# Fused RMSNorm and SiLU on one core: loads and stores alternate between two DMA queues

## The chip, the cores and the metric

The kernel runs on one core of a Trainium2 chip. The metric is the device time of one execution in microseconds (us); less is better. Before the change three executions took 316.88, 316.94 and 317.01 us, a median of 316.94 us. A measurement of this kernel can tell a difference of about 0.2% (0.63 us) from no change.

## The reference

The input x has 8 x 1024 rows of 2048 float32 values, gamma has 2048 values and eps is one number:

```python
rms = np.sqrt(np.mean(x ** 2, axis=-1, keepdims=True) + eps)
out = gamma * x / rms
return (out * (1 / (1 + np.exp(-out)))).astype(np.float32)
```

So each row is scaled by the reciprocal of its root mean square and by gamma, and then goes through SiLU. Input and output are 64 MiB each, and each byte has to cross between the chip's memory and the core's SBUF once.

## The kernel before

**Tiles.** The 8192 rows are cut into 16 blocks of 512 rows. One block is one tile `xt` of 128 partitions x 8192 values (four rows of 2048 values in each partition, `J = 4`), 4 MiB, and the whole block is moved by one DMA in each direction. A partition's part is 32 KB. The pool has six tiles (`BUFS = 6`), so a block's tile can be loaded again only after the store of the block that held it has landed. All the work on a block is done in place in its tile.

**Work on a block.** `squares_scalar` (L65) squares and sums the first one or two rows of each partition on ScalarE (ACT); `squares_vector` (L73) does the others on VectorE (DVE). `share(b)` gives ACT one row in the even blocks 4 to 12 and two elsewhere. `root` (L82, ACT) takes the square root, `invert` (L87, DVE) the reciprocal, `multiply` (L92, DVE) four row products with the reciprocal and gamma, and `silu` (L98, ACT) two halves of SiLU, after which it calls `store`. The last block has its own ending: four products with gamma (L155, DVE), four SiLUs that apply the reciprocal (L157, ACT), and its store.

**Queues.** `load` (L54) issues on ACT's DMA queue, which the profile calls q10 and ACTq. `store` (L102) issues on SyncE's, called q1 and SPq. SyncE (SP) does nothing else but one load of gamma (L110). In each engine instructions run in the order written, and the order is written out by hand (`tc.manual_schedule()`): an instruction that waits holds up all that stand behind it on its engine.

**Order.** Loads 0 to 5 are issued at the start (0 and 1 at once, 2 to 5 after gamma has been spread over the partitions with the help of TensorE). The main loop runs over b = 0 to 14. For b from 3 to 13 an iteration is

```python
squares_scalar(b + 1, loads)   # loads = [b + 3]: issued after the first row's squares
squares_vector(b + 1)
root(b + 1)
multiply(b)
silu(b)                        # ends with store(b)
invert(b + 1)
```

For b < 3 and b = 14 `multiply(b)` comes first and `silu(b)` stands between the two kinds of squares. Load k is issued in iteration k - 3, on ACT, and waits there until the store of block k - 6 has landed.

Of the kernel before, what the change touches and what calls it, by code (L numbers as in the profile page):

```python
# [1 line left out]

# [4 lines left out]

ACT = mybir.ActivationFunctionType
ALU = mybir.AluOpType


@with_exitstack
def kernel(
    ctx: ExitStack,
    tc: tile.TileContext,
    x: bass.AP,
    gamma: bass.AP,
    eps: bass.AP,
    out: bass.AP,
):  # L20

    nc = tc.nc
    P = nc.NUM_PARTITIONS
    f32 = mybir.dt.float32
    x2 = x.flatten_outer_dims()
    o2 = out.flatten_outer_dims()  # L30
    n, d = x2.shape
    J = 4
    BUFS = 6
    nblk = n // (P * J)
    xb = x2.rearrange("(b p j) d -> b p (j d)", p=P, j=J)
    ob = o2.rearrange("(b p j) d -> b p (j d)", p=P, j=J)

    singles = ctx.enter_context(tc.tile_pool(name="singles", bufs=1))
    pool = ctx.enter_context(tc.tile_pool(name="pool", bufs=BUFS))
    small = ctx.enter_context(tc.tile_pool(name="small", bufs=2))  # L40
    psum = ctx.enter_context(tc.tile_pool(name="psum", bufs=1, space=bass.MemoryType.PSUM))

    Q = 4
    w = d // Q
    g = singles.tile([P, d], f32)
    eps_t = singles.tile([P, 1], f32)
    ones = singles.tile([P, P], f32)
    junk_a = psum.tile([P, d], f32, name="junk_a")
    junk_v = psum.tile([P, d], f32, name="junk_v")
    blocks, sss, rmss, rstds = {}, {}, {}, {}  # L50

    def load(b):
        xt = pool.tile([P, J * d], f32, name="xt")
        nc.scalar.dma_start(out=xt, in_=xb[b])  # L54
        blocks[b] = xt

    def row(b, j):
        return blocks[b][:, j * d:(j + 1) * d]

    def squares_scalar(b, loads=()):  # L60


        sss[b] = small.tile([P, J], f32, name="ss")
        for j in range(share(b)):
            nc.scalar.activation(out=junk_a, in_=row(b, j), func=ACT.Square,  # L65
                                 accum_out=sss[b][:, j:j + 1])
            if j == 0:
                for s in loads:
                    load(s)

    def squares_vector(b):
        for j in range(share(b), J):
            nc.vector.tensor_tensor_reduce(  # L73
                out=junk_v, in0=row(b, j), in1=row(b, j), scale=1.0, scalar=0.0,
                op0=ALU.mult, op1=ALU.add, accum_out=sss[b][:, j:j + 1])

    def share(b):
        return 1 if 4 <= b <= 12 and b % 2 == 0 else 2

    def root(b):  # L80
        rms = small.tile([P, J], f32, name="rms")
        nc.scalar.activation(out=rms, in_=sss.pop(b), func=ACT.Sqrt, scale=1.0 / d, bias=eps_t)  # L82
        rmss[b] = rms

    def invert(b):
        rstd = small.tile([P, J], f32, name="rstd")
        nc.vector.reciprocal(out=rstd, in_=rmss.pop(b))  # L87
        rstds[b] = rstd

    def multiply(b):  # L90
        for j in range(J):
            nc.vector.scalar_tensor_tensor(out=row(b, j), in0=row(b, j), scalar=rstds[b][:, j:j + 1],  # L92
                                           in1=g, op0=ALU.mult, op1=ALU.mult)

    def silu(b):
        for h in range(0, J, 2):
            cols = slice(h * d, (h + 2) * d)
            nc.scalar.activation(out=blocks[b][:, cols], in_=blocks[b][:, cols], func=ACT.Silu)  # L98
        store(b)

    def store(b):
        nc.sync.dma_start(out=ob[b], in_=blocks[b])  # L102

    with tc.manual_schedule():

        load(0)
        nc.vector.memset(ones, 1.0)  # L107
        nc.vector.memset(eps_t, float(eps))
        nc.scalar.activation(out=junk_a[:, 0:1], in_=ones[:, 0:1], func=ACT.Square)  # L109
        nc.sync.dma_start(out=g[0:1, :], in_=bass.AP(tensor=gamma.tensor, offset=gamma.offset, ap=[[d, 1], [1, d]]))  # L110
        for c in range(Q):
            cols = slice(c * w, (c + 1) * w)
            nc.tensor.matmul(junk_v[:, cols], ones[0:1, :], g[0:1, cols], start=True, stop=True)  # L113
        load(1)
        nc.vector.tensor_copy(out=g, in_=junk_v)  # L115
        nc.scalar.copy(out=junk_a[:, 0:1], in_=junk_v[:, d - 1:d])  # L116
        for b in range(2, BUFS):
            load(b)

        last = nblk - 1
        SOON = 3
        squares_scalar(0)
        squares_vector(0)
        root(0)
        invert(0)
        for b in range(last):
            loads = [b + 3] if BUFS <= b + 3 < nblk else []
            if b < SOON:  # L130
                multiply(b)
                squares_scalar(b + 1, loads)
                silu(b)
                squares_vector(b + 1)
                root(b + 1)
            elif b < last - 1:
                squares_scalar(b + 1, loads)
# [3 lines that stand above are left out]
                silu(b)  # L141
            else:
                multiply(b)
                squares_scalar(b + 1)
                silu(b)
                squares_vector(b + 1)
                root(b + 1)
            if b + 1 < last:
                invert(b + 1)


        for j in range(J):
            if j == J // 2:
                invert(last)
            nc.vector.tensor_mul(out=row(last, j), in0=row(last, j), in1=g)  # L155
        for j in range(J):
            nc.scalar.activation(out=row(last, j), in_=row(last, j), func=ACT.Silu,  # L157
                                 scale=rstds[last][:, j:j + 1])
        store(last)


# [1 line left out]
_INS = ['x', 'gamma', 'eps']  # L163
_OUTS = [((8, 1024, 2048), 'float32')]

_NUMBERS = {'eps': 9.999999747378752e-06}


# [26 lines left out]
```

## Time and profile before

| | us |
|---|---|
| median of three executions (316.88 to 317.01) | 316.94 |
| span of the profiled execution (its own time is not listed apart; the median is 1.8 longer than the span) | 315.1 |
| DVE busy (75%) | 235.3 |
| ACT busy (68%) | 213.9 |
| PE busy (2%) | 7.2 |
| median of a load from issue to landing, 16 of 4096 KB | 38.7 |
| median of a store from issue to landing, 16 of 4096 KB | 29.0 |
| load 14: issued, landed | 221.2, 259.9 |
| load 15: issued, landed | 240.6, 279.2 |
| store 13: issued, landed | 277.4, 294.9 |
| store 14: issued, landed | 290.3, 304.6 |
| store 15: issued, landed | 300.9, 314.3 |

Read it so: the span is that of one execution under the profiler, and all durations below are of that execution. "DMA share" is the mean busy share of the core's 16 DMA engines; in a short window it can pass 1, because a packet is counted whole in the window in which it starts. A "landing" is the moment at which the transfer's semaphore is complete.

### The profile page before, as it was taken

What the parts mean: (1) busy time and instruction counts of PE and PEld (TensorE: products, weight loads), DVE (VectorE), ACT (ScalarE), POOL (GpSimd) and SP (SyncE); (2) the same over time, 40 slices, a digit from 0 to 9 for tenths busy, and PEclk for the clock granted to TensorE, in tenths of its full rate; (3) what the DMA queues carried; (4) which work ended last, traced back from release to release, by engine and by line L of the source; (5) the groups of instructions that cost most, each with busy time, mean ns of one, the idle gap of its engine ahead of it and who ended that gap; (6) DMA issues with size and microseconds to landing.
All of it is one profiled execution on the core that took longest, in us unless ns stands there. A gap on an engine that the chain in (4) does not pass through costs nothing.

```text
span 315.1 us, 439 instructions
## 1 busy us (share of the span) xinstructions
PE 7.2 (2%) x8; PEld 2.5 (1%) x8; DVE 235.3 (75%) x157; ACT 213.9 (68%) x137; POOL 0.2 (0%) x4
## 2 busy tenths in 40 slices
PE   6200000000000000000000000000000000000000
PEld 2000000000000000000000000000000000000000
DVE  0679697979895695957969489593995939999600
ACT  1269998972799258682687827877278768779910
POOL 0000000000000000000000000000000000000000
DMA  8999999999999999999999999999999999999997
GB/s 334 412 453 416 383 458 408 462 403 462 403 459 408 454 412 458 408 462 403 462 403 462 408 458 408 458 408 458 416 449 416 449 416 449 428 437 428 437 428 308
DMA packets 4613, 134.24 MB, mean 426 GB/s; under 512 B 514, under 2 KB 514, under 8 KB 514
## 3 DMA queue, kind: packets, MB, share of 16 engines
q10 hardware_dynamic: 2304, 67.11, 49.8%
q1 hardware_dynamic: 2306, 67.12, 49.3%
q14 instruction: 3, 0.02, 0.0%
HBM read 67.12 MB, written 67.11 MB: 426 GB/s over the span
## 4 chain that ended last, share of the span: by engine, by line
DMA 68%; DVE 14%; ACT 11%; issue 1%; ACTq 1%; DVEq 0%
DMA xt<-in_x_dram 68%; DVE xt L92 9%; DVE junk_v L73 5%; ACT xt L98 4%; ACT junk_a L65 3%; ACT xt L157 2%; ACT L82 1%; ACTq L190 1%; ACT L157 0%; ACT L98 0%; ACT rms L82 0%; DVE ss L73 0%; ACTq L54 0%; DVE rstd L87 0%; ACT L109 0%
## 5 line engine op out<-in xcount | busy, mean ns | idle before, releaser
L92 DVE SCALAR_TENSOR_TENSOR xt<-xt,rstd,g 128x2048 f32<-128x2048 f32 x60 | 137.0, 2346 | 0.1
L98 ACT ACTIVATE xt<-xt 128x4096 f32<-128x4096 f32 x30 | 108.3, 3615 | 27.4 <-DVE xt L92 27.4
L73 DVE CUSTOM_DVE_ANT_0 junk_v<-xt 128x2048 f32<-128x2048 f32 x37 | 85.1, 2299 | 42.9 <-DMA xt<-in_x_dram 42.2
L65 ACT ACTIVATE junk_a<-xt 128x2048 f32<-128x2048 f32 x27 | 50.7, 1876 | 16.1 <-DMA xt<-in_x_dram 14.0
L82 ACT ACT_TABLE_LOAD x15 | 19.2, 1283 | 26.6 <-DVE ss L73 26.5
L98 ACT ACT_TABLE_LOAD x14 | 18.0, 1283 | 0.2
L115 DVE COPY g<-junk_v 128x2048 f32<-128x2048 f32 x1 | 2.3, 2292 | 9.0 <-PE junk_v L113 9.0
L87 DVE RECIPROCAL rstd<-rms 128x4 f32<-128x4 f32 x16 | 2.7, 172 | 8.4 <-ACT rms L82 8.4
L155 DVE TENSOR_TENSOR xt<-xt,g 128x2048 f32<-128x2048 f32 x4 | 8.9, 2277 | 0.0
L82 ACT ACTIVATE rms<-ss,eps_t 128x4 f32<-128x4 f32 x16 | 4.8, 297 | 5.7 <-DVE ss L73 5.5
L157 ACT ACTIVATE xt<-xt,rstd 128x2048 f32<-128x2048 f32 x4 | 7.7, 1991 | 0.0
L113 PE MATMUL junk_v<-g,ones 1*128 1x512 f32 x8 | 7.2, 1072 | 2.8 <-DMA g<-in_gamma_dram 2.8
L116 ACT COPY junk_a<-junk_v 128x1 f32<-128x1 f32 x1 | 0.1, 144 | 9.8 <-DVE g L115 9.8
L73 DVE DVE_READ_ACCUMULATOR2_ANT ss<- 128x1 f32 x37 | 5.2, 141 | 0.0
L65 ACT ACTIVATION_READ_ACCUMULATOR junk_a<-xt 128x1 f32 x27 | 5.0, 186 | 0.0
L113 PEld LDWEIGHTS junk_v<-g,ones 1*128 1x128 f32 x8 | 2.5, 325 | 5.9 <-issue 5.9
L109 ACT ACT_TABLE_LOAD x1 | 1.3, 1283 | 1.1 <-PEq L176 1.1
L157 ACT ACT_TABLE_LOAD x1 | 1.3, 1283 | 0.0
L107 DVE MEMSET ones<- 128x128 f32 x1 | 0.2, 165 | 0.8 <-PEq L176 0.8
L109 ACT ACTIVATE junk_a<-ones 128x1 f32<-128x1 f32 x1 | 0.2, 174 | 0.0
L176 POOL MEMSET const-bfloat16-1.0<- 128x1 bf16 x1 | 0.1, 103 | 0.0
L176 POOL MEMSET const-uint8-127<- 128x1 uint8 x1 | 0.1, 102 | 0.0
(3 smaller groups left out, 0.3 us busy)
## 6 DMA issues: line engine op xcount, KB each, us to landing
xt<-in_x_dram ACTq DMA_DIRECT2D x16, 4096.0 KB, 38.7
out_dram<-xt SPq DMA_DIRECT2D x16, 4096.0 KB, 29.0
g<-in_gamma_dram SPq DMA_DIRECT2D x1, 8.0 KB
```

Of the source, the lines that this page charges most:

```text
L65: nc.scalar.activation(out=junk_a, in_=row(b, j), func=ACT.Square, accum_out=sss[b][:, j:j + 1])
L73: nc.vector.tensor_tensor_reduce(out=junk_v, in0=row(b, j), in1=row(b, j), scale=1.0, scalar=0.0, op0=ALU.mult, op1=ALU.add, accum_out=sss ...
L82: nc.scalar.activation(out=rms, in_=sss.pop(b), func=ACT.Sqrt, scale=1.0 / d, bias=eps_t)
L87: nc.vector.reciprocal(out=rstd, in_=rmss.pop(b))
L92: nc.vector.scalar_tensor_tensor(out=row(b, j), in0=row(b, j), scalar=rstds[b][:, j:j + 1], in1=g, op0=ALU.mult, op1=ALU.mult)
L98: nc.scalar.activation(out=blocks[b][:, cols], in_=blocks[b][:, cols], func=ACT.Silu)
L109: nc.scalar.activation(out=junk_a[:, 0:1], in_=ones[:, 0:1], func=ACT.Square)
L113: nc.tensor.matmul(junk_v[:, cols], ones[0:1, :], g[0:1, cols], start=True, stop=True)
L115: nc.vector.tensor_copy(out=g, in_=junk_v)
L155: nc.vector.tensor_mul(out=row(last, j), in0=row(last, j), in1=g)
L157: nc.scalar.activation(out=row(last, j), in_=row(last, j), func=ACT.Silu, scale=rstds[last][:, j:j + 1])
L190: with _tile.TileContext(nc) as tc:
```

## The change

Loads of even blocks stay on ACT's queue, loads of odd blocks go over SP's. Stores of odd blocks go over ACT's queue, stores of even blocks stay on SP's. An odd load 7 to 15 is no longer issued among ACT's squares but written after the body of an even iteration: load(b + 5) after `silu(b)` and its store. An even load is issued where it was. So in the program's order load 7 now stands before load 6, load 9 before load 8, and so on.

```diff
     def load(b):
         xt = pool.tile([P, J * d], f32, name="xt")
-        nc.scalar.dma_start(out=xt, in_=xb[b])
+        queue = nc.sync if b % 2 else nc.scalar
+        queue.dma_start(out=xt, in_=xb[b])
         blocks[b] = xt
...
     def store(b):
-        nc.sync.dma_start(out=ob[b], in_=blocks[b])
+        queue = nc.scalar if b % 2 else nc.sync
+        queue.dma_start(out=ob[b], in_=blocks[b])
...
         for b in range(last):
-            loads = [b + 3] if BUFS <= b + 3 < nblk else []
+            loads = [b + 3] if BUFS <= b + 3 < nblk and (b + 3) % 2 == 0 else []
...
+            if b % 2 == 0 and BUFS <= b + 5 < nblk:
+                load(b + 5)
             if b + 1 < last:
                 invert(b + 1)
```

## The prediction

> **What bounds the kernel now.** I read the page's DMA part first, then the packets of each queue in windows, then issues and landings, last the timeline. DMA slices of the page; packets (count, MB, share of 16 engines) by queue from 44 to 310 us, and from 284 to 304:
>
> ```profile
> DMA  8999999999999999999999999999999999999997
> ...
> q1 hardware_dynamic: 2221, 64.91, 56.5%
> q10 hardware_dynamic: 1744, 50.33, 43.8%
> ...
> q1 hardware_dynamic: 316, 8.85, 102.5%
> ```
>
> The shares sum to 100%: the 16 engines never rest, with two queues or with one. From 54 to 64 us q10 shows 80 packets for 60.6%: 0.606 x 160 / 80 = 1.21 us each. A transfer is 128 packets, so 9.7 us alone and 19.4 beside the other queue; 32 transfers are 310.4, and the profile's 315.1 leaves 4.7 for everything else. Nothing that only reorders transfers can gain more than a part of that. Queues share packet by packet, 34 and 32 from 40 to 45 us:
>
> ```profile
> q1 hardware_dynamic: 34, 1.11, 51.6%
> q10 hardware_dynamic: 32, 1.05, 48.5%
> ```
>
> The one place with a loss is where the stores' idle queue joins the busy loads' queue. Store 0 is issued at 35.2; packets from 36 to 38, 38 to 39.5, 39.5 to 40:
>
> ```profile
> L102 SPq DMA_DIRECT2D out_dram<-xt x1: 368/368/368, 35.2 to 35.2; - x1
> ...
> q10 hardware_dynamic: 19, 0.62, 96.6%
> ...
> q10 hardware_dynamic: 13, 0.43, 91.3%
> ...
> q1 hardware_dynamic: 14, 0.46, 212.3%
> ```
>
> The first store packet comes 4.4 us after the issue, and the load packets ahead of it last 0.966 x 32 / 19 = 1.63 and 0.913 x 24 / 13 = 1.69 us: 32 packets, 0.45 too long each, over 16 engines 0.9 us lost. Without the loss the delay is 3.5.
>
> Compute has slack (DVE 75%, ACT 68% busy) except at the end, from load 14's landing at 259.9:
>
> ```profile
> 260.02 2.30 DVE L73 CUSTOM_DVE_ANT_0 junk_v<-xt 128x2048 f32<-128x2048 f32 x1 [5.52 <-DMA xt<-in_x_dram]
> 264.62 9.13 DVE L92 SCALAR_TENSOR_TENSOR xt<-xt,rstd,g 128x2048 f32<-128x2048 f32 x4
> 273.88 9.14 DVE L92 SCALAR_TENSOR_TENSOR xt<-xt,rstd,g 128x2048 f32<-128x2048 f32 x4
> 279.23 1.88 ACT L65 ACTIVATE junk_a<-xt 128x2048 f32<-128x2048 f32 x1 [1.82 <-DMA xt<-in_x_dram]
> ```
>
> Block 14's squares, products of 13, products of 14, squares of 15 run back to back on DVE; stores 13, 14, 15 are issued 17.5, 30.4, 41.0 us after the landing. Each still finds its predecessor under way (14 lands at 304.6, 15 is issued at 300.9), so this chain is hidden, by about 2.5 us.
>
> **The change, part by part.**
>
> *Issues.* ACT issues 16 transfers before and after (0.33 us each), SP 16 and gamma. On ACT eight loads become stores, which stand behind their silu: 8 x 0.4 = 3 us, at nothing, because ACT will wait longer for a load (below); uncovered it would be those 3 us.
>
> *Start.* Loads 1, 3, 5 come from SP at once; the engines are full anyway. Load 0 now shares with load 1 and lands near 22.5 instead of 12.9, 2 and 3 near 42, 4 and 5 near 62.5. Cover: stores 0 and 1 now stand in the queues behind loads 5 and 4, and cannot start before 61. Block 0's products start 5.9 us after its landing, 15.7 per block follow (37.0 and 52.7 in the timeline), silu ends 13 after: stores ready at 41, 57, 73. In time: store 2 is due at 80.5. The price if that cover were gone, block 0's 9.6 us, is not on the path.
>
> The skill's page DMA: Bandwidth & Descriptors (Queues, rings and completion order) says that an engine drains about 9 to 17 descriptors of one ring before it switches; load 0's 8 packets per engine would then go first, and it would land near 13. The rows above show turns of one packet, and I go by them; the end would not move by either.
>
> *Who waits for whom.* In the program's order load 7 takes its tile before load 6, so the tiles swap. The built order shows it: load 6 waits for store 1 (was 0), 8 for 3, 10 for 5, 12 for 7, 14 for 9; 7 for 0, 9 for 2, and so on. So an even load waits for the store directly ahead of it in ACT's own queue: that queue must run dry and its landing be known (last packet to landing 1.65 us: one packet of the other queue, 1.21, and the 0.4 that store 15 shows alone, whose last packet ends at 313.9 and which lands at 314.3) before the load is issued, and then it joins a busy queue: 3.5. A gap of 5.2 us, five times. SP's queue fills the gaps, so the engines stay busy, but ACT's queue falls behind SP's. ACT stands at the load meanwhile; behind it are root and silu of the odd block and thus its store, and DVE's next reciprocal. From such an issue: root 1.6, table 1.3, silu 7.2: odd store after 10.2; squares 4.1, root 1.6, table 1.3, silu 7.2: even store (SP) after 24.8.
>
> *The walk*, at 1.21 us a packet, 16 packets per cycle in each queue. Stores 0 and 1 run from 61.1 to 80.5, load 6 is issued at 82.2 and starts at 85.7. SP's queue (store 2, load 7, store 4, load 9) is not empty in this cycle: 5.2 + 2 x 19.4 = 44.0, load 8 issued at 126.2. From then on SP's queue runs dry for a while before each even store, and ACT's goes alone. One cycle in full: store 4 and load 9 (16 packets) follow load 7 at 114.1; 4.3 packets go beside store 3 until 124.5, 4.3 alone in ACT's gap until load 8 starts at 129.7, and the other 7.4 beside load 8 take 17.9, to 147.6. Load 8 has then had 7.4 of its 8 and ends at 148.3. Store 5 (ready at 136.4) goes alone until store 6 joins: ready at 126.2 + 24.8 = 151.0, started at 154.5; that is 5.1 packets, and the last 2.9 beside store 6 take 7.0, to 161.5. Landing and issue: load 10 at 163.2. In the same way load 12 at 203.2 and load 14 at 241.0. Load 14 lands 3.5 + 19.4 + 1.65 later, at 265.5 against 259.9. Check by work: before its last packet at 263.9, ACT's queue has moved 13 transfers and SP's 13.9: 26.9 x 9.7 + 2.9 = 263.8. At most 14 are ready on SP's side (store 12 is ready at 265.8), so this is near its latest; 13.4 would give 259.
>
> *The end.* Store 13 is issued at 283.0. Store 12, alone since 279, ends at 284: a gap of up to 1. Block 15's squares need not wait for its load (landed 267), so store 14 comes 29.3 after the landing, at 294.8, and 15 after 40.0, at 305.5. Store 14 finds the engines empty. Alone, a load took 12.2 from issue to landing: store 14 lands at 307.0, and 15 between 9.7 later (316.7) and 305.5 + 12.2 (317.7); I take 317.2. Before: 314.3. The sum is +2.9; the rest around the last landing stays (2.6 up to the median): 316.94 + 2.9 = **319.8 us**.
>
> *Joins.* Loads 6, 8, 10, 12, 14 join a running queue, and stores 6, 8, 10 join on SP's side: eight until load 14 lands. Price of one: 0, as for a transfer whose queue is running, to 0.9, as for store 0, the nearest row, which was however also the first store. A gain is excluded: a packet's time did not fall under 1.21. I take the low end with store 0's own loss kept, because its slowed packets may belong to the first store; the high end, 8 x 0.9 = 7.2 less the 0.9 of store 0, goes into the range: 326.
>
> The same page (Issuing engines are not separate DMA queues) speaks against any effect: DMAs of both issuers interleave on the same 16 engines, and a second issuer saves only issue time. That gives 316.9 by itself. The full shares above agree with it for the rate; it says nothing of who stands behind whom, from which my sum comes.
>
> **Rivals.**
> - *Dear joins*: as above, 321.5 to 326. For: the only join in the trace cost 0.9. Against: it was the first store.
> - *Not slower*: the engines never rest, so only the end can lose. If load 14 lands by 262.4, store 15 is issued by 302.4, one us before its predecessor ends at 303.4, and store 14 too is in time; the end stays at 314.3, and without store 0's loss (its queue is never empty now) comes to 313.4: 316.0 to 317.5. It needs SP's queue to have moved 13.6 transfers or less by then, that is store 10 ready some 4 us later or ACT's gaps shorter. Deciding point: 262.4.
> - *Does not do what it says*: excluded, the built order has the loads and stores on both queues.
>
> **Numbers.** My case (318 to 321.5) 0.52, dear joins 0.28, not slower 0.20, of which faster by over 0.2% (what a measurement can tell) 0.07 and within it 0.13. The range 316.8 to 326.0 leaves out the faster part and the top of the dear joins.
>
> **What would show it.** Load 8 issued near 126 and load 14 near 241, ACT idle 10 us before odd silus, load 14 landed at 265 with 15 close behind, DMA share below 1 only after 283: right. Packets over 1.3 us at each join: dear joins. Load 14 before 262.4, or DMA gaps in the middle: my walk is wrong.

## The result, and the profile after

The changed kernel takes 321.17 us (median of four executions, 320.61 to 321.91) against 316.91 us for the kernel before on the same chip: a ratio of 1.0135, 95% interval 1.0123 to 1.0147, or 4.3 us more. The prediction was 319.8 us in a range of 316.8 to 326.0, slower with a chance of 0.8.

Ratios and intervals leave out executions over 1.5% above the fastest of their kernel, which one experiment had.

On reading the times: a profile is of one of the timed executions, and the time of each execution is its own span plus a nearly constant rest, 1.7 to 1.8 us here and in most kernels below, 1.9 to 2.2 in "all but the start" and in the alternating kernels with halved stores. But in the kernels whose loads and stores alternate the executions differ by 1 us and more. So a trace stands for its own execution, and the medians are what counts for totals. The profile after is of the slowest of the four executions, 321.91 us, which is 5.0 us above the kernel before.

The DMA slices of the page after (tenths of the engines' time in 40 equal slices of the span):

```profile
DMA  8999999999999999999999999999999999989797
```

The engines are as full as before for 35 slices; the holes are all in the last five. Busy time of the units in stretches (columns: stretch and its length, PE, PEld, DVE, ACT and POOL busy with counts, granted clock, DMA share, GB/s), first two of the kernel before, then the kernel after:

```profile
80.00:276.00 196.00, 0.00 (x0) 0.00 (x0) 154.10 (x102) 138.27 (x84) 0.00 (x0) 1.00 1.00 433
276.00:300.00 24.00, 0.00 (x0) 0.00 (x0) 20.46 (x13) 22.09 (x14) 0.00 (x0) 1.00 1.00 430
```

```profile
80.00:276.00 196.00, 0.00 (x0) 0.00 (x0) 152.60 (x102) 132.17 (x84) 0.00 (x0) 1.00 1.00 431
276.00:300.00 24.00, 0.00 (x0) 0.00 (x0) 23.93 (x14) 21.91 (x12) 0.00 (x0) 1.00 0.86 366
...
280.00:284.00 4.00, 0.00 (x0) 0.00 (x0) 3.96 (x3) 3.09 (x2) 0.00 (x0) 1.00 0.93 401
284.00:288.00 4.00, 0.00 (x0) 0.00 (x0) 4.00 (x3) 3.57 (x3) 0.00 (x0) 1.00 0.70 287
...
296.00:300.00 4.00, 0.00 (x0) 0.00 (x0) 4.00 (x2) 3.95 (x4) 0.00 (x0) 1.00 0.64 270
```

From 284 to 300 us DVE and ACT are busy nearly all the time and the DMA engines have gaps: the compute of the last blocks is no longer hidden. Of the 5.0 us of this execution 24 x 0.14 = 3.4 lie between 276 and 300 us, 0.9 in the middle (196 us at 431 instead of 433 GB/s), and the rest behind 300 us.

Load 14's landing and the chain behind it, from the timeline (start, duration, instruction, in brackets the idle time before it and what ended it):

```profile
268.31 2.30 DVE L74 CUSTOM_DVE_ANT_0 junk_v<-xt 128x2048 f32<-128x2048 f32 x1 [6.49 <-DMA xt<-in_x_dram]
...
272.92 9.13 DVE L93 SCALAR_TENSOR_TENSOR xt<-xt,rstd,g 128x2048 f32<-128x2048 f32 x4
...
282.18 9.14 DVE L93 SCALAR_TENSOR_TENSOR xt<-xt,rstd,g 128x2048 f32<-128x2048 f32 x4
...
285.74 0.35 ACTq L104 DMA_DIRECT2D out_dram<-xt  x1
...
308.16 0.34 ACTq L104 DMA_DIRECT2D out_dram<-xt  x1
```

It is the chain of before, begun 8.3 us later (load 14 lands at 268.2, before at 259.9). Store 13 goes out 17.5 us after the landing, store 15 40.0 after it, at 308.2, and alone it needs 11.1 us to land: 319.3, against 314.3 before.

Why load 14 is late shows in ACT's waits, in the timeline at load 8

```profile
126.13 0.34 ACTq L55 DMA_DIRECT2D xt<-in_x_dram  x1
126.55 1.28 ACT L83 ACT_TABLE_LOAD   x1 [15.66 <-DMA out_dram<-xt]
```

and in the list of waits (who waited for what: us in total, times, longest):

```profile
ACT L83 <- DMA out_dram<-xt: 41.1, 3, 15.7
ACT L83 <- DVE xt L93: 14.2, 1, 14.2
```

ACT stands for 15.7 us at load 8 until store 3 has landed, and 14.1, 11.4 and 14.2 us at loads 10, 12 and 14 (the last is put down to DVE, but load 14 is issued at 245.1, within 0.1 us of store 9's landing). Meanwhile ACT's queue runs dry. Packets by queue from 124.6 to 129.6 us (the four on q10 carry no data, they only tell of the end of store 3):

```profile
q1 hardware_dynamic: 77, 2.20, 101.7%
q10 hardware_dynamic: 4, 0.00, 0.0%
```

### The profile page after: what moved, and what is told of

Read it like the earlier page. It is cut to its first block, busy times and chain, and to the rows that moved or that the text cites. A ratio compares the mean times of both kernels' runs of the same rounds, so it can differ in the third digit from the quotient of the medians.

```text
span 320.1 us, 440 instructions
## 1 busy us (share of the span) xinstructions
PE 7.2 (2%) x8; PEld 2.5 (1%) x8; DVE 235.7 (74%) x157; ACT 212.9 (67%) x137; POOL 0.2 (0%) x4
## 3 DMA queue, kind: packets, MB, share of 16 engines
q10 hardware_dynamic: 2304, 67.11, 48.9%
## 4 chain that ended last, share of the span: by engine, by line
DMA 51%; DVE 26%; ACT 16%; issue 3%; ACTq 0%; DVEq 0%
DMA out_dram<-xt 37%; DVE xt L93 16%; DMA xt<-in_x_dram 14%; ACT xt L99 9%; DVE junk_v L74 9%; ACT L83 2%; ACT xt L161 2%; DVE xt L159 1%; ACT L99 1%; ACT rms L83 1%; ACTq L55 0%; DVE ss L74 0%; DVE rstd L88 0%; ACTq L104 0%; ACTq L83 0%
## 5 line engine op out<-in xcount | busy, mean ns | idle before, releaser
L83 ACT ACT_TABLE_LOAD x15 | 19.2, 1283 | 58.9 <-DMA out_dram<-xt 41.1
```

## The experiments

Theory: the end of the kernel is set by load 14's landing, and that is late because an even load waits for the store directly ahead of it in ACT's own queue, so that the queue runs dry and falls behind. Rivals: the mixed start; queues that carry both directions, or that join a running queue; ACT's standing still.

**Tiles handed over in block order.** Both queues still alternate; only the odd loads keep their old place in the program.

```diff
-            loads = [b + 3] if BUFS <= b + 3 < nblk and (b + 3) % 2 == 0 else []
+            loads = [b + 3] if BUFS <= b + 3 < nblk else []
...
-            if b % 2 == 0 and BUFS <= b + 5 < nblk:
-                load(b + 5)
```

> Both queues alternate as in the changed kernel, but odd loads keep their old place in the program, so tiles are handed over in block order: load 6 waits for store 0, load 8 for store 2 (both on SP's queue), load 7 for store 1. Theory (an even load waits for the store directly ahead of it in its own queue, falls behind, and the tail after load 14 is exposed): ACT's queue no longer runs dry, load 14 lands near 261.6 instead of 268.2, the engines stay full to the end, 316.9 us (316.4 to 317.6). Rival (queues that mix loads and stores, or ACT issuing stores, cost by themselves): 320 to 322 as the changed kernel.

Measured: 317.67 us, ratio 1.0031 (1.0016 to 1.0046). In the profile, of an execution of 319.05 us, load 14 lands at 261.9:

```profile
261.94 1.88 ACT L66 ACTIVATE junk_a<-xt 128x2048 f32<-128x2048 f32 x1 [4.98 <-DMA xt<-in_x_dram]
...
301.90 0.34 ACTq L104 DMA_DIRECT2D out_dram<-xt  x1
```

So 3.5 of the 4.3 us belong to the swapped tiles by the medians (3.3 by the ratios), and alternating queues as such, with ACT issuing half the stores, cost 0.7 (0.5 to 1.5 by the interval). The order in each queue is the same in this kernel as in the changed one; what is gone is the dry time: between 87 and 280 us ACT's queue is never without a data packet for more than 1.6 us, against 5.1 to 5.3 at loads 8 to 14 in the changed kernel. The 0.7 is a small miss. The profiled execution, which took 2.1 us more than the kernel before, shows where it lost them: the engines are full until 312, but the last store, issued at 301.9, lands at 316.4 only. Packets of its queue in two windows (count, MB, share), from 313 to 314.5 and from 314.5 to 316.2:

```profile
q10 hardware_dynamic: 17, 0.07, 10.7%
...
q10 hardware_dynamic: 2, 0.03, 4.5%
```

In the first 15 engines finish (15 of the 17 packets are those that tell of the end), in the second one engine alone moves one more data packet. In the kernel before all 16 finish within 0.9 us.

**The last three stores in halves**, in the changed kernel and as a control in the kernel before (there the same edit on the `nc.sync` line):

```diff
             nc.scalar.activation(out=blocks[b][:, cols], in_=blocks[b][:, cols], func=ACT.Silu)
-        store(b)
+            if b >= 13:
+                store(b, cols)
+        if b < 13:
+            store(b)
...
-    def store(b):
+    def store(b, cols=slice(None)):
         queue = nc.scalar if b % 2 else nc.sync
-        queue.dma_start(out=ob[b], in_=blocks[b])
+        queue.dma_start(out=ob[b][:, cols], in_=blocks[b][:, cols])
...
                                  scale=rstds[last][:, j:j + 1])
-        store(last)
+            if j % 2:
+                store(last, slice((j - 1) * d, (j + 1) * d))
```

> The changed kernel, with the stores of blocks 13, 14 and 15 cut in two halves, each issued as soon as its half of the SiLU is done. Theory (of the 5 us lost, over 4 are idle DMA engines after 283 us, waiting for the last three blocks' compute): store 13 starts near 281, the last half at 308 lands some 4.9 us earlier than the whole store did, 316 to 317.5 us. Rival (the loss lies in the middle, in queues that join a running one or in packets that got slower): at most 1 us gained, 320 us or more.

> Control: the kernel before with the same halved last stores. Theory (the engines are full to the end there, the tail's compute is hidden): no change, 316.5 to 317.3 us. Rival (the last store's own latency is what the halving shortens, in any kernel): 2 to 5 us less, 312 to 315 us.

Measured: 319.57 us (ratio 1.0079, 1.0064 to 1.0093), 1.6 less than the changed kernel, between the two expectations; the control 317.25 us (1.0009, 1.0001 to 1.0018), no gain. In the trace of the first the holes at the end are gone:

```profile
284.00:288.00 4.00, 0.00 (x0) 0.00 (x0) 4.00 (x2) 3.56 (x4) 0.00 (x0) 1.00 0.98 418
...
296.00:300.00 4.00, 0.00 (x0) 0.00 (x0) 4.00 (x4) 3.59 (x5) 0.00 (x0) 1.00 0.99 426
```

This execution took 318.85 us, 3.1 less than the one profiled of the changed kernel, yet the medians differ by half of that: there the profile caught the slowest of four executions, here the second fastest of six. So I ran both again side by side.

> The changed kernel once more, beside the next one, for a second profile: 320.6 to 322 us, load 14 lands 267 to 269, 4 to 5 us of idle DMA engines after 283 us. If the middle rather than the end differs from one execution to the next, load 14's landing moves by over 1 us between the two profiles.

> The changed kernel with the halved last stores once more: its first profile had under 1 us of idle engines at the end and a span 3.4 us shorter, but its time was only 1.6 us shorter. Theory (the end's idle time is the loss): 316.5 to 318.5 us beside the changed kernel, and the first timing was an exception. Rival (the engines run out of step with one another, so that landings come late though the engines are busy, and halves give back only a part): 319 to 320 us again.

Measured: 321.48 us (ratio 1.0140, 1.0119 to 1.0160) and 318.92 us (1.0066, 1.0052 to 1.0081): 2.6 less, with spans of 319.4 and 316.6, and again between the two expectations. Load 14 lands at 267.5 in the changed kernel's second profile, 0.7 earlier than in the first, and the last store and the whole execution (321.21 us) are 0.7 earlier too. So the engines' waiting for the last stores is part of the loss, some 1.6 to 2.6 us of it; with the halves 2.0 to 2.6 us above the kernel before are left.

**The start alone.** The kernel before, with loads 1, 3 and 5 on SP.

```diff
-        nc.scalar.dma_start(out=xt, in_=xb[b])
+        queue = nc.sync if b in (1, 3, 5) else nc.scalar
+        queue.dma_start(out=xt, in_=xb[b])
```

> The kernel before with only loads 1, 3 and 5 moved to SP's queue; all else as before. Block 0 lands near 21.5 instead of 12.9 and store 0 stands behind load 5, from 61 us. Theory (the engines are full meanwhile, the late start is hidden): 316.9 us (316.4 to 317.6). Rival (the first block's delay of some 9 us is not won back): 320 us or more. On the 0.9 us that were lost when the stores' queue first joined: if it is the join, store 0 follows load 5 in a running queue and the loss is gone, 316.0; if it is the first store, it stays.

Measured: 317.28 us, ratio 1.0012 (1.0004 to 1.0021). Block 0's squares begin 7.3 us later (20.4 instead of 13.1), and it costs 0.3 us.

**All but the start.** The changed kernel with loads 0 to 5 on ACT.

```diff
-        queue = nc.sync if b % 2 else nc.scalar
+        queue = nc.sync if b % 2 and b >= BUFS else nc.scalar
```

> The changed kernel, but loads 0 to 5 all stand on ACT's queue as before; from block 6 on everything alternates, with the swapped tiles. Theory (the even load that waits for the store ahead of it in its own queue, and the exposed end): the same loss as the changed kernel, 320 to 322 us; load 6 comes later (near 91, store 1 stands behind load 5), load 8 near 119, load 10 near 163. Rival (the mixed start, with store 0 not before 61 us, is the loss): about 317 us.

Measured: 323.47 us, ratio 1.0197 (1.0170 to 1.0224). The loss is there without the mixed start, and 1.5 us above what I had given: load 6 came at 95.3, load 10 at 166.3, load 14 landed at 270.6. Together the two runs clear the start. The profiled execution, the slowest of four at 324.42 us, shows one more thing: packets in the middle that are long again. From 120 to 125 us, where SP's queue resumes after being empty from 102 to 120, they take 1.170 x 80 / 65 = 1.44 us each against 1.21, 0.9 us in all:

```profile
q1 hardware_dynamic: 65, 2.13, 117.0%
```

From 144 to 146 us 20 packets of 1.81 us cost another 0.7. What makes them long at these two places is not shown.

**The stores' queues exchanged.**

```diff
-        queue = nc.scalar if b % 2 else nc.sync
+        queue = nc.sync if b % 2 else nc.scalar
         queue.dma_start(out=ob[b], in_=blocks[b])
```

> The changed kernel with the stores' queues exchanged: even stores on ACT's queue, odd ones on SP's. Loads, their order and the swapped tiles are as in the changed kernel, so load 6 still waits for store 1, load 8 for store 3 and so on, but that store is now on the other queue and an even store stands ahead of the load in its own. Theory (what costs is a queue that runs dry while its next load waits for its own last store): ACT's queue stays filled, load 14 lands some 4 us earlier than in the changed kernel, 317 to 318.2 us. Rival (the swap as such costs, as an even load waits for a store one block later wherever that is, or ACT's standing still): 320 to 322 us.

Measured: 326.89 us, ratio 1.0341 (1.0299 to 1.0382). Here the theory, as I had put it, fell. The queues do not run dry: between 61 and 276 us neither is without a data packet for more than 1.7 us, which is no more than in the kernel before (1.9). Packets by queue from 80 to 280 us:

```profile
q10 hardware_dynamic: 1504, 44.04, 51.0%
q1 hardware_dynamic: 1472, 42.47, 49.2%
```

Load 14's issue and block 14's squares in its timeline, and its stretch from 284 us:

```profile
239.32 0.35 ACTq L55 DMA_DIRECT2D xt<-in_x_dram  x1
...
273.31 2.30 DVE L74 CUSTOM_DVE_ANT_0 junk_v<-xt 128x2048 f32<-128x2048 f32 x1 [8.76 <-DMA xt<-in_x_dram]
```

```profile
284.00:292.00 8.00, 0.00 (x0) 0.00 (x0) 7.96 (x6) 7.09 (x3) 0.00 (x0) 1.00 0.15 66
```

But each even load now stands behind one more store in its queue (six even ones, 0 to 10, stand ahead of load 14 instead of five odd ones, 1 to 9), so load 14, issued 5.8 us earlier than in the changed kernel, needs 33.9 us to land instead of 23.1. It lands at 273.2, and from 284 to 292 us there is next to nothing to move. The rival is not right either: its times, 320 to 322, were passed by 5 us, though from load 8 on ACT stands only some 3 us at a load, less than it has to wait there for DVE's squares anyway (up to 5.3). A dry queue is one way to make load 14 late; a store ahead of it is another. How much of the changed kernel's loss is the dry time itself, and how much that its even loads wait for a store one block later, no run here separates, since undoing the swap undoes both. What load 14's landing means for the end, in five traces:

| kernel, its profiled execution | load 14 lands | last store lands | difference |
|---|---|---|---|
| before | 259.9 | 314.3 (engines full to the end) | 54.4 |
| changed | 268.2 | 319.3 | 51.1 |
| changed, again | 267.5 | 318.6 | 51.1 |
| all but the start | 270.6 | 321.6 | 51.0 |
| stores' queues exchanged | 273.2 | 324.2 | 51.0 |

**The last two loads in block order.** If it is load 14 alone, it should be enough to mend that one.

```diff
-            loads = [b + 3] if BUFS <= b + 3 < nblk and (b + 3) % 2 == 0 else []
+            loads = [b + 3] if BUFS <= b + 3 < nblk and (b + 3 == last or b % 2) else []
...
-            if b % 2 == 0 and BUFS <= b + 5 < nblk:
+            if b % 2 == 0 and BUFS <= b + 5 < last:
```

> The changed kernel, but only the last two loads in block order: load 15 stands in the program after load 14 (still on SP's queue), so load 14 takes the tile of store 8 and no longer waits for store 9, the last store ahead of it in ACT's queue. All cycles before it are as in the changed kernel. New theory, from load 14's landing and the last store's in the four traces of changed order (268.2 and 319.3, 267.5 and 318.6, 270.6 and 321.6, 273.2 and 324.2): the last store lands 51.1 us after load 14, unless the full engines end later (314.3). Load 14 should land near 264 (store 9's end at 243.5, 19.4 beside SP's queue, 1.2 to the landing), the last store at 315.1, 317 to 318.5 us. Rival (what costs is spread over all cycles, or is the queue that runs dry as such): 320 to 321 us.

Measured: 320.58 us (319.52 to 323.06), ratio 1.0132 (1.0102 to 1.0162). The median fits the rival. The profile is of the second fastest of six executions, 319.81 us: load 14 lands there at 264.9, 0.9 later than expected, and the last store at 317.1, 2.0 later, after 12.3 us instead of 11.1, with the end of the store before it still under way. So load 14's landing alone does not set the end, and what the slower executions lost beyond this one no trace shows.

**The halves on top of block order**, for the last pair alone and for all:

> Only the last two loads in block order (320.58 us, where load 14 landed at 264.9 in the profile but the timed executions came out longer than that) and the last three stores in halves. Theory (the end's idle time is the loss, and load 14's landing differs between executions): 317 to 318.5 us, with a smaller spread than without the halves (319.5 to 323.1). Rival (a loss in the middle of the timed executions that the profile did not catch): 319.5 us or more.

> All tiles in block order (as in the first experiment, 317.67 us) and the last three stores in halves. In that profile the engines had 0.4 us of idle time left at the end, but finished the last store up to 2.9 us apart. If what is left of the loss is the end's idle time: 317.3 us. If it is the engines being out of step: 317.0 to 317.7 us with executions still spread over 1 us or more. Faster than the kernel before (under 316.3): no theory expects it.

Measured: 320.82 us (ratio 1.0108, 1.0077 to 1.0140) and 318.94 us (1.0067, 1.0047 to 1.0086; two of its seven executions took 325.57 and 334.58 us). Neither is better than its kernel without the halves (320.58 and 317.67), the second is worse by 1.3 us. So waiting for whole stores at the end was not what these two had left, and no kernel here beats the one before. The trace of the first, of an execution of 320.58 us, shows where most of it lies there: the engines are full until 312 us and then finish apart, some of them after 316, where in the kernel before all have finished by 314. The stretch from 314 us:

```profile
314.00:318.00 4.00, 0.00 (x0) 0.00 (x0) 0.00 (x0) 0.00 (x0) 0.00 (x0) 1.00 0.12 53
```

**A tiny store first.** The kernel before, to see what the 0.9 us are that are lost when the stores begin.

```diff
+        nc.sync.dma_start(out=ob[nblk - 1][:, 0:P], in_=ones)
         load(1)
```

> The kernel before, with a 64 KB store of the tile of ones into the last block's rows issued on SP right after gamma; store 15 overwrites it later. Some 0.8 us of engine time are lost in every trace when the first store starts, beside a queue that joins (before) or in a running one (after). If the first store of an execution costs that once, and the start hides it: 316.0 to 316.3 us. If it is the change from loads alone to loads beside stores, or anything that comes again: 316.9 to 317.2 us, with the long packets again at 36 us.

Measured: 317.09 us, ratio 1.0004 (0.9996 to 1.0013), and the long packets came again: q10 from 36 to 38 us with 1.115 x 32 / 25 = 1.43 us each, against 1.21.

```profile
q10 hardware_dynamic: 25, 0.82, 111.5%
```

So being the first store of an execution is not what costs it.

## Why the prediction was right, and where its sizes were off

The direction and the mechanism held, and the walk can be checked against the trace step by step. The sum was low: 2.9 us were forecast and 4.3 measured, near the upper end of what the prediction gave its own case (318 to 321.5). The trace is of an execution that lost 5.0.

- **Full engines, nothing to gain.** Held: no reordering got under 316.9 us.
- **The start hidden.** Held: load 0 landed at 21.5 us (22.5 forecast; with turns of eight packets it would have been near 13), block 0 was ready late, its store stood in the queue anyway, and the start alone costs 0.3 us.
- **ACT's issues.** Each odd store delays ACT by 0.4 us, as said, beside 55 us of standing at loads (41.1 and 14.2 in the waits).
- **The swapped tiles.** Held, and shown by undoing them: 3.5 of 4.3 us by the medians. That they cost it by way of the dry queue is read from the trace; its own share no run isolates.
- **The gaps.** Forecast were five of 5.2 us in ACT's queue; data packets are missing there for 4.3 us before load 6 and for 5.3, 5.3, 5.1 and 5.2 before loads 8 to 14.
- **The walk.** Loads 8, 10, 12, 14 were forecast at 126.2, 163.2, 203.2, 241.0 and came at 126.1, 166.7, 204.4, 245.1; load 14 landed at 268.2 instead of 265.5. The term that was mis-sized is the landing: I took 1.65 us from last packet to landing, as if the 16 engines kept step. They don't in this kernel: the end packets of stores 5, 7 and 9, for which loads 10, 12 and 14 wait, are spread over 4.4, 4.7 and 6.5 us. Store 5's first engine is done at 161.9, where 161.5 was forecast for all, and its last at 166.3. Load 14's 16 end packets are spread over 2.9 us (264.7 to 267.7), where the kernel before has under 0.9 (258.6 to 259.5). A landing counts the last engine. Not all of the delay was handed on: from load 10 to load 12 it took 37.8 us instead of the 40.0 forecast, and without that the error would have been larger.
- **The end.** Stores 13, 14, 15 were forecast 17.5, 29.3 and 40.0 us after load 14's landing and came 17.5, 29.0 and 40.0 after it. A lone store needed 11.1 us, not the 12.2 of the first load, which gave back 0.6: the last landing came at 319.3 instead of 317.2.
- **Joins.** The dear joins did not come in the changed kernel. From 80 to 276 us the engines moved 431 GB/s against 433 before, 196 x 2 / 433 = 0.9 us for all eight joins and everything else, a tenth of a us each. (In "all but the start" one place where a queue resumed had the whole 0.9.) The 0.9 us at the beginning of the stores are there in the changed kernel too (from 58 to 59.5 us 16 packets of 0.935 x 24 / 16 = 1.40 us, from 59.5 to 61 16 of 1.80: 0.8 us), where store 0 follows load 5 in a running queue. So this loss needs neither a join nor an execution's first store; in every trace long packets cost 0.5 to 1.0 us between 30 and 64 us, where the first stores come in.
- **The rival not slower** had its deciding point at 262.4 for load 14's landing. The kernel with tiles in order passed it (261.9), but that execution took 319.05 us and the median was 317.67, above what that rival had (316.0 to 317.5). The point looked only at the compute behind load 14; that the engines finish apart was not in it.

In the Trainium skill, the page DMA: Bandwidth & Descriptors (Issuing engines are not separate DMA queues) says that DMAs of different issuers interleave on the same engines and that a second issuer saves only issue time. By that alone the sum would have been no change, 316.9 us. For the rate the trace agrees: the two queues' shares after, 49.0% and 48.9%, add up to 98%, and no kernel gained by the second issuer. The 4.3 us lie in who waits behind whom.

## What to carry to other kernels

In a kernel that the DMA engines bound, moving transfers between queues moves no bytes faster; ask what stands ahead of the last loads in their queue, and whether the compute behind the last load still has stores left to hide under. When loads change their place in the program, check which tile each now gets and thereby which store it waits for: here one swapped pair per two blocks cost 3.5 of 4.3 us. A load that waits for the store directly ahead of it in its own queue empties that queue each time, here for about 5 us. And when the executions of a kernel differ, ask which of them the profile shows before a sum is checked against it.

## What the runs showed of the hardware that was not expected

- The 16 engines share two queues packet by packet and need not keep step, and a transfer is as late as its last engine: from first to last end packet it is under 0.9 us in the kernel before, 2.9 us for load 14 and 6.5 for store 9 in the changed one. Where the queues did not run dry from 61 to 276 us (stores' queues exchanged) it stayed at 0.8. A dry queue is not the only way, though: with the tiny store it was 0.9 to 2.2 us.
- The changed kernel repeats worse: five executions lie between 319.94 and 322.48 us, eleven of the kernel before beside them between 316.69 and 317.24. That the spread comes from the engines being out of step is likely, but no run here isolates it: the kernel with the stores' queues exchanged, in step in its trace, took 326.75 to 326.99 us in five executions and 331.30 in a sixth.
- A 4 MiB store alone takes 11.1 us from issue to landing in four traces, the kernel's first load 12.2. About half of the difference is that the first packets of an execution are slower: in the kernel before 14 packets from 1.5 to 2.5 us take 1.597 x 16 / 14 = 1.83 us each, against 1.21 later.
